# Scheduling the six score products of an attention block as one group over two PSUM banks

## The chip, the cores and the metric

The kernel runs on one core of a Trainium2 chip. The metric is the device time of one execution in microseconds (us), and of several runs the median. The engines are called PE (TensorE, matrix products), DVE (VectorE), ACT (ScalarE), POOL (GpSimd) and SP (which issues the transfers). PE writes its products into PSUM, and a bank of PSUM holds one result of 128 x 512 fp32 numbers. In the lines of the profile, `sc<-qg,qg 64*128 64x512 f16` is a product: into tile `sc`, from two tiles `qg`, 64 rows deep, with 128 columns of weights and 512 moving columns.

## What is computed

The reference is a bidirectional encoder trunk of two layers on 512 tokens of width 1024. Each layer projects the tokens into three groups of heads (differential softmax attention, a gated linear recurrence in both directions, and cross-attention into a memory of 256 tokens), joins them in one output projection and a layer norm, and then runs a gated MLP with a depthwise convolution and a second layer norm. The change concerns the first group:

```python
def diff_attention(q, k, v, lam):          # 4 heads, two components c of width 64 each
    ...
        s = jnp.einsum('bqhcd,bkhcd->bhcqk', qi, k).astype(jnp.float32)
        p = jax.nn.softmax(s, axis=-1)
        a = p[:, :, 0] - lam * p[:, :, 1]
        return jnp.einsum('bhqk,bkhv->bqhv', a.astype(v.dtype), v)
    ...
def hybrid_layer(x, mem, cos, sin, layer, ...):
    proj = x @ w_in
    ...
    mix = jnp.concatenate([da_o, hg_o, mx_o], axis=-1) @ w_out
    x = layer_norm(DEEPNORM_ALPHA * x + mix, ln1_g, ln1_b)
    ...
```

Each head has two score matrices, one per component of width 64, and the second softmax is taken from the first with a weight.

## The kernel before

**Products in three parts.** A number is split into a high and a low fp16 half, and each large product is made of three fp16 products that add up in one PSUM bank: high by high, high by low and low by high (`mm3`, L269, through `mm`, L132; so all of them carry L137 in the profile). Weights arrive as fp32 in tiles `wst` and are scaled and split by ACT and DVE into `wh` and `wl` (`prep`, L250 to L267).

**The score blocks.** `da_attn` (L963) handles two heads of a layer: 2 heads x 4 blocks of 128 queries, so eight blocks, and with two layers and two head pairs there are four such stretches. `scores(i)` (L967) takes two PSUM tiles of tag "sc", one for each component, and writes six products into them: three parts (L978), and for each part the two components (L979 to L981). Component 0 reads rows 0 to 63 of the tiles `qg` and component 1 rows 64 to 127, so one uses the upper and one the lower half of the rows of the array. In program order the two row halves alternate. Then DVE takes the negative maximum of each component (L983) and scales both (L984), and ACT takes the exponentials with their sums (L986), which reads the banks for the last time. `finish` (L989) subtracts the second softmax (L995, DVE), turns the result by four transposes on PE (L996, through L473), and ACT copies it (L997); `values` (L999) multiplies with the values after four blocks.

**What lies beside them.** While a stretch runs, PE also has the projections of the next heads (`gemm_f` and `gemm_t`, tiles `mm<-wh,xh` or `mm<-xh,wh`) and the output products (`down_part`, L514: six products into a tile "mm" for two slices of 128 rows, after which DVE adds the tile to the residual stream, L529; tiles `mm<-wh,mgh`). There are two banks of tag "mm", three of "sc" and two of "tr" (L122).

**What sets the order.** The program is traced once, and a planner then decides the order of the instructions on each engine and which bank each tile gets (`make_plan`, L1520). `extract` (L1232) turns each instruction into an `Op` with a cost in us, the instructions that it depends on, and the list `tiles` of the tiles that it reads or writes. A product with 64 fp16 rows is given a cost of 0.005 us if it follows one on the other row half in program order, and the ordinary cost of 0.216 us otherwise (L1267 to L1275); this is settled before the order is. `deadlines` (L1484) gives PE's instructions due times: the sum of PE's costs in program order; other engines' due times follow from these. `simulate` (L1341) then walks through time. Banks of a tag are handed to tiles in program order (`assign`, L1383). An instruction is offered to its engine once all tiles in its list have a bank and all that it depends on is done (`ntile` and `npred`); of the instructions offered, an engine takes the one that is due first (L1435). A tile's bank goes back when all instructions that list it are done (L1470 to L1477). The order is then fixed by links from each instruction to the next on its engine, and the engines work through it in that order on the chip, each waiting for the data and banks that it needs.

Of the kernel before, what the change touches and what calls it, by code (L numbers as in the profile page):

```python
# [1158 lines left out]
def _esize(dt):  # L1159
    s = str(dt)  # L1160
    return 4 if "32" in s else 2 if "16" in s else 1


def _n(ap):
    n = 1
    for _, c in list(ap)[1:]:
        n *= c
    return n


class Op:
    __slots__ = ("i", "name", "eng", "cost", "tail", "reads", "writes", "table", "preds", "succs", "tiles", "dmab", "line", "kind", "small", "order_ins", "mv", "istr")


def cost_of(i, kind, eng, outs, ins):
# [56 lines left out]
def extract(instrs):  # L1232
    ops = []
    last_half = None
    for i in instrs:
        kind = type(i).__name__
        if kind.startswith("BassTile"):
            continue
        o = Op()
        o.i = len(ops)  # L1240
        o.name = i.name
        o.eng = ENG[str(i.engine).split(".")[-1]]
        o.kind = kind
        o.line = i.debug.lineno if i.debug else 0
        get = lambda xs: [a.bass_ap for a in xs if "AccessPattern" in type(a).__name__]
        outs, ins = get(i.outs), get(i.ins)
        o.order_ins = ins
        o.mv = ins[0] if ins else None
        o.istr = bool(getattr(i, 'is_transpose', False))
        o.table = 0  # L1250
        if kind == "InstActivation":
            o.table = SETS.get(str(i.func).split(".")[-1], 0)
        o.dmab = 0
        if o.eng == "SP":
            b = outs[0]
            n = _esize(b.dtype)
            for _, c in list(b.ap):
                n *= c
            o.dmab = n
            o.cost, o.tail = 0.06, 0  # L1260
        else:
            o.cost, o.tail = cost_of(i, kind, o.eng, outs, ins)
        o.reads = [b for b in ins if type(b.tensor).__name__ == "Tile"]
        o.writes = [b for b in outs if type(b.tensor).__name__ == "Tile"]
        o.preds, o.succs = set(), []
        o.small = _n(outs[0].ap) <= 16 if outs else False
        if o.eng == "PE" and "float16" in str(ins[0].dtype) and ins[0].ap[0][1] == 64:  # L1267
            half = ins[0].offset // ins[0].ap[0][0]
            if last_half not in (None, half):
                o.cost = 0.005  # L1270
                last_half = None
            else:
                last_half = half
        elif o.eng == "PE":
            last_half = None  # L1275
        ops.append(o)

    cache = {}

    def region(b):  # L1280
        t = b.tensor
        es = _esize(b.dtype)
        ap = tuple(tuple(x) for x in b.ap)
        key = (b.offset, ap, es, t.name if False else 0)
        r = cache.get(key)
        if r is None:
            stride = ap[0][0]
            p0, f0 = divmod(b.offset, stride) if stride else (0, b.offset)
            pos = {f0}
            for s, c in ap[1:]:  # L1290
                if s == 0:
                    continue
                pos = {x + s * q for x in pos for q in range(c)}
            m = 0
            if len(pos) == max(pos) - min(pos) + 1:
                lo, n = min(pos) * es, len(pos) * es
                m = ((1 << n) - 1) << lo
            else:
                w = (1 << es) - 1
                for x in pos:  # L1300
                    m |= w << (x * es)
            r = cache[key] = (p0, p0 + ap[0][1], m)
        return r

    hist = defaultdict(list)
    tiles = {}
    for o in ops:
        o.tiles = []
        for wr, bs in ((False, o.reads), (True, o.writes)):
            for b in bs:  # L1310
                t = b.tensor
                nm = t.name
                if nm not in tiles:
                    tiles[nm] = t
                if nm not in o.tiles:
                    o.tiles.append(nm)
                psum = "PSUM" in str(t.space)
                p0, p1, m = region(b)
                h = hist[nm]
                for (j, w2, a0, a1, m2) in h:  # L1320
                    if (wr or w2) and j != o.i:
                        if psum or (a0 < p1 and p0 < a1 and m & m2):
                            o.preds.add(j)
        for wr, bs in ((False, o.reads), (True, o.writes)):
            for b in bs:
                p0, p1, m = region(b)
                h = hist[b.tensor.name]
                psum = "PSUM" in str(b.tensor.space)
                if wr:
                    if psum:  # L1330
                        h[:] = []
                    else:
                        h[:] = [e for e in h if not (p0 <= e[2] and e[3] <= p1 and (e[4] & ~m) == 0 and e[0] != o.i)]
                h.append((o.i, wr, p0, p1, m))
    for o in ops:
        for p in o.preds:
            ops[p].succs.append(o.i)
    return ops, tiles


# [179 lines left out]
def make_plan(instrs):  # L1520
    ops, tiles = extract(instrs)
    _, _, _, order, slot_of = simulate(ops, tiles, deadlines(ops, tiles))
    return list(order.values()), {tiles[t].source_name: s for t, s in slot_of.items()}
# [45 lines left out]
```

## Time and profile before

| what | us |
|---|---|
| median of 3 runs | 1530.95 |
| lowest and highest of them | 1530.77, 1532.63 |
| the profiled execution | 1531.64 |
| its span, from the first to the last instruction | 1529.9 |

The profile is of one execution. A timeline line has the start, the length, the engine, the line of the code, the operation, the tiles, the shape and a count of like instructions merged into one; in square brackets stand the idle time of the engine before it and the instruction whose end it waited for. A line that groups instructions ends with the time in which at least one of them ran, the mean length of one in ns, and the idle time just before them. Products are pipelined, so that one starts before the one ahead of it has ended: the distance of two starts is what a product costs PE, not its length. A line of the view by windows has the window, its length, the busy time and number of instructions of each engine in it, the granted TensorE clock, the share of time in which the transfer engines were busy, and what they moved.

### The profile page before, as it was taken

The page shows a single profiled execution, that of the slowest core. Times are in us where ns is not written, and L with a number is a line of the kernel's source. Part 1 is how long each engine was busy: PE and PEld are TensorE (multiplying, and loading weights), DVE is VectorE, ACT ScalarE, POOL GpSimd, SP SyncE. Part 2 cuts the span into 40 slices and gives each one's busy share as a digit, 9 for nine tenths or more (in the row PEclk, how much of TensorE's full clock was granted, in tenths as well). Part 3 has the DMA queues.
Part 4 walks back from the last instruction along what each step waited for, and adds up shares of the span by engine and source line. Part 5 has one row for each costly group of instructions (what it writes and reads, how often), then busy time and mean ns, then how long its engine had stood idle before and what let it go on. Part 6 is the DMA issues. An engine that isn't in the chain of part 4 may idle for free. (4 is left out here: it accounts for less than half of the span.)

```text
span 1529.9 us, 24770 instructions
## 1 busy us (share of the span) xinstructions
PE 1477.0 (97%) x10072; PEld 824.3 (54%) x10072; DVE 1147.8 (75%) x2133; ACT 862.1 (56%) x1090; POOL 233.7 (15%) x258
## 2 busy tenths in 40 slices
PE   4999999999999999999999999999999999999997
PEld 3766565464574444444478475655555544444443
DVE  7688967778797766775794969668779776676677
ACT  4776566656376555554556555566653756455550
POOL 4131312030011000010110331021201101001001
PEclk9999999999999999999999999999999999999999
DMA  6332221132233233233234312111232433343321
GB/s 217 126 118 84 71 70 56 56 108 75 69 111 110 88 105 110 83 110 103 91 111 139 97 43 84 50 61 56 67 99 62 133 111 91 102 111 94 100 83 55
DMA packets 158141, 141.93 MB, mean 93 GB/s; under 512 B 3286, under 2 KB 139082, under 8 KB 158026
## 3 DMA queue, kind: packets, MB, share of 16 engines
q1 hardware_dynamic: 158026, 140.34, 29.5%
q8 instruction: 79, 1.29, 0.4%
q14 instruction: 36, 0.29, 0.1%
HBM read 138.23 MB, written 2.10 MB: 92 GB/s over the span
## 5 line engine op out<-in xcount | busy, mean ns | idle before, releaser
L137 PEld LDWEIGHTS <-wh 128*128 128x128 f16 x2688 | 256.5, 98 | 232.1 <-issue 2.3
L266 DVE SCALAR_TENSOR_TENSOR wl<-wst,ws,wh 128x2048 f16<-128x2048 f32 x122 | 315.9, 2590 | 73.0 <-ACT wh L265 72.9
L137 PE MATMUL mm<-xh,wl 128*128 128x512 f16 (+1 forms) x832 | 301.7, 363 | 1.3 <-DVE wl L266 1.3
L137 PE MATMUL mm<-xh,wh 128*128 128x512 f16 (+1 forms) x832 | 301.7, 363 | 0.0
L137 PE MATMUL mm<-xl,wh 128*128 128x512 f16 (+1 forms) x832 | 301.4, 363 | 0.0
L262 ACT ACTIVATE wh<-wst 128x2048 bf16<-128x2048 f32 x122 | 232.2, 1903 | 110.2 <-PE stat L165 54.1
L265 ACT ACTIVATE wh<-wst,ws 128x2048 f16<-128x2048 f32 x122 | 243.5, 1996 | 41.6 <-DVE wi L156 25.6
L137 PE MATMUL mm<-wh,t 128*128 128x512 f16 (+1 forms) x768 | 223.1, 370 | 1.7 <-DVE z L529 1.6
L137 PEld LDWEIGHTS <-wl 128*128 128x128 f16 x1344 | 131.4, 98 | 123.3 <-issue 1.9
L137 PEld LDWEIGHTS <-t 128*128 128x128 f16 x1152 | 110.4, 98 | 122.2 <-issue 1.2
L529 DVE SCALAR_TENSOR_TENSOR z<-mm,inv,z 128x512 f32<-128x512 f32 x176 | 130.3, 745 | 47.1 <-PE mm L137 33.3
L137 PE MATMUL sc<-xh,wh 128*128 128x512 f16 (+1 forms) x448 | 156.2, 349 | 1.3 <-ACT xh L247 0.8
L137 PE MATMUL sc<-xl,wh 128*128 128x512 f16 (+1 forms) x448 | 156.2, 349 | 0.0
L137 PE MATMUL sc<-xh,wl 128*128 128x512 f16 (+1 forms) x448 | 156.2, 349 | 0.0
L137 PE MATMUL mm<-wl,t 128*128 128x512 f16 (+1 forms) x384 | 142.1, 370 | 0.0
L1098 POOL TENSOR_TENSOR t<-f 128x512 f32<-128x512 f32 x44 | 58.4, 1328 | 545.3 <-DVE f L1096 429.3
L152 DVE TENSOR_SCALAR we<-stat 128x1 int32<-128x1 int32 x122 | 18.4, 151 | 125.2 <-PE stat L165 125.1
L137 PE MATMUL mm<-wh,mgh 128*128 128x512 f16 x192 | 72.8, 379 | 5.1 <-DVE z L529 2.5
L1094 ACT ACTIVATE f<-sc,cvb,cw 128x512 f32<-128x512 f32 x44 | 34.1, 775 | 71.4 <-PE stat L165 68.8
L137 PE MATMUL mm<-wh,mgl 128*128 128x512 f16 x192 | 72.6, 380 | 0.6 <-DVE gi L156 0.6
L137 PE MATMUL mm<-wl,mgh 128*128 128x512 f16 x192 | 72.8, 379 | 0.0
L137 PE MATMUL mm<-wh,xh 128*128 128x256 f16 x256 | 67.6, 281 | 2.7 <-ACT xh L247 2.7
(224 smaller groups left out, 2188.3 us busy)
## 6 DMA issues: line engine op xcount, KB each, us to landing
wst<-in_w_up_dram SPq DMA_DIRECT2D x88, 512.0 KB, 4.5
wst<-in_w_in_dram SPq DMA_DIRECT2D x36, 1024.0 KB, 5.1
wst<-in_w_down_dram SPq DMA_DIRECT2D x22, 1024.0 KB, 5.0
wst<-in_w_out_dram SPq DMA_DIRECT2D x12, 1024.0 KB, 5.1
wst<-in_w_mem_kv_dram SPq DMA_DIRECT2D x8, 1024.0 KB, 5.7
z<-in_x_dram SPq DMA_DIRECT2D x4, 512.0 KB, 9.6
mix<-in_ln_g_dram SPq DMA_DIRECT2D x4, 512.0 KB
mix<-in_ln_b_dram SPq DMA_DIRECT2D x4, 512.0 KB
```

Source lines behind the costliest of these rows:

```text
L137: T.matmul(o, lhsT, rhs, start=start, stop=stop)
L152: V.tensor_scalar(e, tot.bitcast(I32), 0x7F000000, 1, ALU.bitwise_and, ALU.logical_shift_right)
L262: A.activation(h.rearrange("p a b -> p (a b)").bitcast(BF16), flat, AF.Square, accum_out=ss)
L265: A.activation(h.rearrange("p a b -> p (a b)"), flat, AF.Identity, scale=s)
L266: V.scalar_tensor_tensor(l.rearrange("p a b -> p (a b)"), flat, s, h.rearrange("p a b -> p (a b)"), ALU.mult, ALU.subtract)
L529: V.scalar_tensor_tensor(zs, p_, ivs[half % len(ivs)], zs, ALU.mult, ALU.add)
L1094: A.activation(c, p_, AF.Identity, scale=cw[:, 1, v : v + 1], bias=cvb[:, l, i + 22 * v : i + 22 * v + 1])
L1098: G.tensor_tensor(gt[:, n, :], c2[:, 0, :], c2[:, 1, :], ALU.mult)
```

## The change

The six products of a block get the same list of tiles: both "sc" tiles of the block. So in the planner none of them is offered to PE before both tiles have a bank, and each tile's bank goes back only when all six are done (and its readers). `Op` gets a field for the row half, and the rule for the cost is written in another way with the same result. A new pass at the end of `extract` goes through PE's instructions in program order, gathers runs of products that have a row half, and joins the lists of tiles in groups of six. Instructions, their operands and what they compute stay the same.

```diff
@@ class Op
-    __slots__ = ("i", "name", "eng", "cost", ..., "order_ins", "mv", "istr")
+    __slots__ = ("i", "name", "eng", "cost", ..., "order_ins", "mv", "istr", "half")
@@ def extract
-        if o.eng == "PE" and "float16" in str(ins[0].dtype) and ins[0].ap[0][1] == 64:
-            half = ins[0].offset // ins[0].ap[0][0]
-            if last_half not in (None, half):
-                o.cost = 0.005
+        o.half = None
+        if o.eng == "PE":
+            if "float16" in str(ins[0].dtype) and ins[0].ap[0][1] == 64:
+                o.half = ins[0].offset // ins[0].ap[0][0]
+                if last_half not in (None, o.half):
+                    o.cost, last_half = 0.005, None
+                else:
+                    last_half = o.half
+            else:
                 last_half = None
-            else:
-                last_half = half
-        elif o.eng == "PE":
-            last_half = None
         ops.append(o)
...
     for o in ops:
         for p in o.preds:
             ops[p].succs.append(o.i)
+    run = []
+    for o in ops + [None]:
+        if o is not None and o.eng != "PE":
+            continue
+        if o is not None and o.half is not None:
+            run.append(o)
+            continue
+        for k in range(0, len(run), 6):
+            both = list(dict.fromkeys(t for p in run[k : k + 6] for t in p.tiles))
+            for p in run[k : k + 6]:
+                p.tiles = both
+        run = []
     return ops, tiles
```

More of the change, by code (lines that the diff above doesn't have):

```diff
@@ L1171 @@
 class Op:
-    __slots__ = ("i", "name", "eng", "cost", "tail", "reads", "writes", "table", "preds", "succs", "tiles", "dmab", "line", "kind", "small", "order_ins", "mv", "istr")
+    __slots__ = ("i", "name", "eng", "cost", "tail", "reads", "writes", "table", "preds", "succs", "tiles", "dmab", "line", "kind", "small", "order_ins", "mv", "istr", "half")
 def cost_of(i, kind, eng, outs, ins):
```

## The prediction

> **What bounds the kernel now.** I read the page first, for which engine is full, and then asked the trace for the products that the change names.
>
> ```profile
> span 1529.9 us, 24770 instructions
> PE 1477.0 (97%) x10072; PEld 824.3 (54%) x10072; DVE 1147.8 (75%) x2133; ACT 862.1 (56%) x1090; POOL 233.7 (15%) x258
> ```
>
> TensorE is busy for 1477.0 of 1529.9 us, VectorE for three quarters. Work taken from PE is therefore worth its own length wherever other work is ready to move up; the question is where it is not. The groups by shape give the score products, the only ones with 64 rows:
>
> ```profile
> L137 PE MATMUL sc<-qg,qg 64*128 64x512 f16 x192 | 49.6, 379 | 0.8 <-ACT f L986 0.7
> ```
>
> 192 products are 32 blocks of six (2 layers x 2 head pairs x 8 blocks). They lie in four stretches, each opened by a run of nine. The timeline of PE at the first, and the last of these four runs:
>
> ```profile
> 271.51 1.47 PE L137 MATMUL sc<-qg,qg 64*128 64x512 f16 x9
> 272.91 0.28 PE L137 MATMUL mm<-wh,xh 128*128 128x256 f16 x1
> ...
> 277.93 0.82 PE L137 MATMUL sc<-qg,qg 64*128 64x512 f16 x3
> 278.68 0.28 PE L137 MATMUL mm<-wh,xh 128*128 128x256 f16 x1
> ...
> 1084.31 1.47 PE L137 MATMUL sc<-qg,qg 64*128 64x512 f16 x9
> ```
>
> Nine products hold PE from 271.51 to 272.91, 1.40 us, but three alone hold it for 0.75 (277.93 to 278.68). So the first six of the nine took 0.65 us, 0.22 a pair: they alternated and ran two at a time. The last three are one row half of the second block, because there are three "sc" banks and the first block took two. All later products come in such groups of one half, which cost as much as six would. The groups' busy time confirms the count: four runs at 1.47 and 52 halves at 0.82 make 48.5 us, against 49.6 in the row. The 1.1 us left over are halves cut in two by a transpose, as here:
>
> ```profile
> 290.22 0.39 PE L137 MATMUL mm<-wh,mgh 128*128 128x512 f16 x1
> 290.54 0.60 PE L137 MATMUL sc<-qg,qg 64*128 64x512 f16 x2
> 291.08 0.66 PE L473 MATMUL tr<-cst,f 128*128 128x128 f32 x4
> 291.66 0.39 PE L137 MATMUL sc<-qg,qg 64*128 64x512 f16 x1
> 291.98 0.39 PE L137 MATMUL mm<-wl,mgh 128*128 128x512 f16 x1
> ```
>
> Such a half is busy 0.60 + 0.39 instead of 0.82, 0.17 more, so there are about seven. Only 4 of 32 blocks alternate today.
>
> **The change part by part.** It touches no instruction, only the planner's input: each of a block's six products now lists both PSUM banks, so none is offered to PE before both are free. The costs (0.216 us for the first of a pair, 0.005 for the second) are as before; the plan already charged a block about 0.66 us, and paid for two lone halves on the chip. Due times come from program order and move by one product at most, so I expect the order far from the score blocks to stay much as it is.
>
> *What PE saves.* The price of a lone half, at the end of the first stretch:
>
> ```profile
> 300.99 0.38 PE L137 MATMUL mm<-wh,mgh 128*128 128x512 f16 x1
> 301.21 0.38 PE L137 MATMUL mm<-wl,mgh 128*128 128x512 f16 x1
> ...
> 301.88 0.38 PE L137 MATMUL mm<-xl,wh 128*128 128x512 f16 x1
> 302.19 0.82 PE L137 MATMUL sc<-qg,qg 64*128 64x512 f16 x3
> 302.94 0.39 PE L137 MATMUL mm<-xh,wl 128*128 128x512 f16 x1
> ```
>
> Ordinary products start 0.22 us apart (300.99, 301.21). Before the half there are 0.31, so entering costs 0.09; from its start to the next product there are 0.75. A lone half takes 0.84 us of PE, a block of two 1.69. Six alternating products take 0.65 between their own starts plus about 0.10 on leaving and 0.09 on entering: 0.84 again. A block that now alternates saves 0.84 us. In each stretch six blocks save that. The second block saves 0.65, since its first half now rides behind the run of six without an entry or exit of its own. That is 5.7 us a stretch, 22.8 for four. The seven cuts cost about 0.2 each (one more entry and exit), 1.4; I assume that few new ones arise, since the group is no longer on PE than a half is now. The sum is **24.2 us of PE**.
>
> *What hides it or takes its place.* The other work of the four stretches, from the second block on:
>
> ```profile
> core 0: us, PE busy (x) PEld busy (x) DVE busy (x) ACT busy (x) POOL busy (x), PEclk, DMA share, GB/s
> 278.00:303.00 25.00, 25.00 (x116) 9.41 (x117) 20.12 (x47) 17.45 (x34) 0.00 (x0) 1.00 0.09 30
> 343.00:369.00 26.00, 25.76 (x130) 10.67 (x128) 20.81 (x51) 19.40 (x38) 0.00 (x0) 1.00 0.19 68
> 1024.00:1052.00 28.00, 27.71 (x146) 12.96 (x145) 23.46 (x58) 19.44 (x36) 0.00 (x0) 1.00 0.15 49
> 1088.00:1116.00 28.00, 27.27 (x155) 13.65 (x153) 22.07 (x55) 20.01 (x38) 0.00 (x0) 1.00 0.18 62
> sum 107.00, PE 105.74 PEld 46.70 DVE 86.46 ACT 76.30 POOL 0.00; mean PE 26.43 PEld 11.68 DVE 21.62 ACT 19.08 POOL 0.00
> ```
>
> PE is full here (105.7 of 107), VectorE is the next engine with 86.5. If the same work stays in the stretches they cannot go under 86.5 us: the saving is at most 20.5 of the 24.2, and only with VectorE never idle. How full it gets beside a full PE, two windows show:
>
> ```profile
> 360.00:370.00 10.00, 9.84 (x43) 3.33 (x41) 9.53 (x21) 5.61 (x11) 0.00 (x0) 1.00 0.33 108
> 370.00:380.00 10.00, 8.08 (x53) 5.69 (x53) 9.73 (x24) 5.26 (x9) 0.60 (x2) 1.00 0.53 140
> ```
>
> At 95% of VectorE PE was still full (9.84), at 97% it lost a fifth (8.08). So I take 95%: 86.46 / 0.95 = 91.0 us, a saving of **16 us**. The ends that I keep are 24.2 (fillers that need little VectorE move in, and its work moves out of the stretches) and nothing.
>
> *The wait that is added.* Now the first half of a block starts when one bank is free, and its maximum (L983) is taken while PE does the other half later. With the change both halves wait for the exponential of the block before to free a second bank, and both maxima come after it. The chain in the trace, a half's start to its bank's release:
>
> ```profile
> 282.58 0.69 DVE L983 TENSOR_REDUCE dam<-sc 128x1 f32<-128x512 f32 x1 [0.43 <-PE sc L137]
> ...
> 283.01 0.82 PE L137 MATMUL sc<-qg,qg 64*128 64x512 f16 x3
> ...
> 283.57 0.78 ACT L986 ACTIVATE f<-sc,dam,iqk 128x512 f32<-128x512 f32 x1 [1.08 <-DVE dam L984]
> ...
> 283.87 0.69 DVE L983 TENSOR_REDUCE dam<-sc 128x1 f32<-128x512 f32 x1 [0.33 <-PE sc L137]
> ```
>
> and the group that reads the exponential's sum out, in the view by lines:
>
> ```profile
> L986 ACT ACTIVATION_READ_ACCUMULATOR f<-sc,dam,iqk 128x1 f32 x11 | 2.1, 195 | 0.0
> ```
>
> The products take 0.86 us (283.01 to 283.87), maximum to exponential 0.99 (282.58 to 283.57), the exponential with its sum 0.78 + 0.20: 2.8 us now, and about 3.5 with the second maximum in line. The blocks follow each other at (302.19 - 277.93) / 6 = 4.04 us. The longer chain fits into that pitch with 0.5 us to spare, so I cost it at nothing beside VectorE's limit. Behind the waiting product PE's whole queue stands, but the plan puts other products ahead of the group; what that costs if there is none is the fourth rival.
>
> The sum is made against the profiled execution's 1531.64 us (its span is 1529.9): 1531.64 - 16 = 1515.6. The median of the runs, 1530.95, lies 0.7 below that execution, so I predict **1515 us**.
>
> **The rivals.**
>
> *All of it.* PE finds fillers that need little of VectorE (projections rather than output products), and VectorE's work spreads beyond the stretches: 1530.95 - 24.2 = 1507. For it: VectorE now idles for maxima that PE delivers late:
>
> ```profile
> L983 DVE TENSOR_REDUCE dam<-sc 128x1 f32<-128x512 f32 x12 | 8.3, 691 | 6.6 <-PE sc L137 6.5
> L529 DVE SCALAR_TENSOR_TENSOR z<-mm,inv,z 128x512 f32<-128x512 f32 x7 | 5.2, 746 | 0.1
> ```
>
> (the first stretch). Against it: the fillers are mostly output products, and each six of them (1.30 us of PE) end in a 0.75 us eviction by VectorE. Chance 0.20.
>
> *The banks' readers become the bound.* The longer chain keeps today's waiting in VectorE's and ScalarE's queues, 4.04 - 2.8 = 1.2 us a block, and the pitch grows to about 4.7. PE's freed time must then be filled with output products whose evictions wait in the same VectorE queue. About a third of 24.2 is kept, 8 us: 1523. Against it: VectorE idles for 20.5 of 107 us today. Chance 0.20. The Trainium skill, "TensorEngine Tiling (Array Packing)", section "PSUM Bottleneck", states such a rule: packing the array speeds TensorE up but not the emptying of PSUM, which may then be the limit. No run so far shows it for these blocks.
>
> *It does not do what it says.* If transposes or other products come between the halves in the plan, a block pays two entries again and the pair's overlap is lost; with all blocks cut, nothing changes: 1531. Against it: the six become ready together and PE takes the earliest due, which is the other half each time, as the four opening blocks show. Chance 0.05.
>
> *Slower.* The pitch grows by 0.65 us and PE finds nothing to do in the freed 0.84 + 0.65 = 1.49 us of each block, because the two "mm" banks wait for L529 behind the score work. Where PE idles for more than 0.84 / 1.49 = 56% of that, the block is longer than now. At 75% it costs 28 x (0.75 x 1.49 - 0.84) = 7.8 us: 1539. For it, at the end of the last stretch:
>
> ```profile
> 1120.17 0.38 PE L137 MATMUL mm<-wh,mgh 128*128 128x512 f16 x1 [1.92 <-DVE z L529]
> ```
>
> Against it: this is the longest such wait in the stretches, and after the second one output products remain in stock that need no score of it:
>
> ```profile
> L137 PE MATMUL mm<-wh,mgl 128*128 128x512 f16 x28 | 10.6, 379 | 0.0
> L137 PE MATMUL mm<-wh,mgh 128*128 128x512 f16 x28 | 10.6, 379 | 0.6 <-DVE z L529 0.6
> L137 PE MATMUL mm<-wl,mgh 128*128 128x512 f16 x28 | 10.6, 379 | 0.0
> ```
>
> (370 to 400 us): 84 at 0.22 are 18 us. Chance 0.05.
>
> **How the numbers follow.** The forecast, 1510 to 1520, has 0.50; all of it, to 1506, has 0.20; the readers, 1520 to 1528, have 0.20; no change and slower have 0.05 each. The first three are all faster by more than 0.2% (3 us, about what a measurement of this kernel can tell from no change): 0.90 faster, 0.05 within, 0.05 slower. The range 1506 to 1526 takes in the first two cases and most of the third, and leaves out a little more than one in ten.
>
> **What would show it.** The 64-row products should stand in about 32 runs of six that hold PE for 0.75 us each from first start to the next product, their busy time falling from 49.6 us to some 26 to 28. The four stretches should be 3 to 5 us shorter each, with VectorE at 90% or more. If PE shows new gaps that end with L986 or L529 in them, the readers have taken the gain; if VectorE stays near 80% and PE near 100%, all of it has come. The prediction is wrong if the plan reorders work far from the stretches, or if VectorE cannot keep 95% because its maxima now come in pairs.

## The result and the profile after

| | us, median (lowest to highest) | profiled execution | its span | mean granted clock |
|---|---|---|---|---|
| before | 1531.15 (1530.77 to 1532.63), 4 runs | 1531.64 | 1529.9 | 0.997 |
| after | 1519.86 (1518.66 to 1522.45), 4 runs | 1518.81 | 1517.0 | 0.993 |

After takes 0.9927 of the time of before (95% interval 0.991 to 0.9944): 11.3 us less. That is inside the range of the prediction, and 4.7 us less of a gain than the 16 that it forecast.

The page of after, its span and its busy times:

```profile
span 1517.0 us, 24771 instructions
PE 1458.1 (96%) x10072; PEld 823.6 (54%) x10072; DVE 1148.1 (76%) x2133; ACT 860.2 (57%) x1090; POOL 237.2 (16%) x258
```

PE is busy for 18.9 us less than before (1477.0), and the span is 12.9 shorter. So some 6 us are new time in which PE stands idle. The score products, in the groups by shape:

```profile
L137 PE MATMUL sc<-qg,qg 64*128 64x512 f16 x192 | 28.4, 380 | 0.4 <-ACT f L986 0.3
```

Their busy time fell from 49.6 to 28.4 us. Of the 32 blocks 27 stand in one uncut run of six. The timeline of PE in the first stretch shows how six now cost what three did:

```profile
276.85 0.82 PE L137 MATMUL sc<-qg,qg 64*128 64x512 f16 x6
277.60 0.28 PE L137 MATMUL mm<-wh,xl 128*128 128x256 f16 x1
...
281.30 0.82 PE L137 MATMUL sc<-qg,qg 64*128 64x512 f16 x6
```

From 276.85 to the next product there are 0.75 us, for six products as before for three. The stretches themselves, in the view by windows, one window for each:

```profile
core 0: us, PE busy (x) PEld busy (x) DVE busy (x) ACT busy (x) POOL busy (x), PEclk, DMA share, GB/s
277.00:307.00 30.00, 28.30 (x174) 14.67 (x171) 28.79 (x67) 21.86 (x39) 1.74 (x1) 1.00 0.31 103
340.00:372.00 32.00, 27.20 (x156) 15.80 (x152) 27.57 (x65) 21.69 (x39) 0.00 (x0) 0.89 0.28 88
1018.00:1049.00 31.00, 30.15 (x180) 14.99 (x179) 29.04 (x68) 21.92 (x39) 2.71 (x3) 1.00 0.23 81
1078.00:1110.00 32.00, 28.75 (x181) 15.39 (x177) 29.45 (x66) 22.19 (x41) 1.20 (x2) 1.00 0.31 101
sum 125.00, PE 114.40 PEld 60.85 DVE 114.85 ACT 87.67 POOL 5.65; mean PE 28.60 PEld 15.21 DVE 28.71 ACT 21.92 POOL 1.41
```

VectorE is at 92% (114.85 of 125) and PE at 91.5%, where before PE had 99% and VectorE 81%. What PE waits for, in the view of the waits, before and then after (in all, how often, longest):

```profile
PE mm L137 <- DVE z L529: 4.1, 5, 1.9
```

```profile
PE mm L137 <- DVE z L529: 9.1, 8, 2.7
...
PE tr L243 <- DVE xl L248: 1.9, 1, 1.9
```

**The books.** Gaps between PE's instructions add up to 34.9 us before and 41.6 after. And the granted clock fell to half in two places where before it did not. One window at each, after:

```profile
364.00:371.00 7.00, 6.03 (x30) 5.91 (x30) 4.98 (x13) 2.81 (x6) 0.00 (x0) 0.52 0.82 229
1148.00:1153.00 5.00, 4.23 (x15) 2.08 (x15) 3.83 (x6) 1.37 (x2) 0.00 (x0) 0.66 0.00 0
```

In the records the clock is at half for 6.8 us at the first and 3.4 us at the second. PE is busy in 9.3 of these 10.2 us (the rest is idle time, counted above), and half of that, 4.6 us, is lost. (One further 3.4 us at half speed both kernels have, before at 172 us and after at 77.) So: 23.5 us less PE work, 6.7 more idle, 4.6 more lost to the clock, 0.6 gained ahead of PE's first instruction: 23.5 - 6.7 - 4.6 + 0.6 = 12.8, against 12.9 in the spans. The 23.5 is not measured by itself: it is what the busy time leaves, 18.9 + 4.6. The score products alone show most of it. From each one's start to the next product's start, without idle time, they hold PE for 45.5 us before and 26.1 after, 19.4 less, and the 25 entries that are saved (62 groups before, 37 after), at the 0.09 us of the prediction, add 2.3.

**Where it was lost.** The start of the same product (the k-th of its kind) in both traces, for five places; each figure is the later kernel's time less that of before. Three of the experiments below stand beside it. Each column is one execution, and the four executions of after differ by up to 3.8 us.

| the place, by its time in before | after | e2 | e3 | e9 |
|---|---|---|---|---|
| ahead of stretch 1, 268.14 | -0.7 | -0.6 | -0.7 | 0.0 |
| behind stretch 1, 314.56 | -5.1 | -5.1 | -0.7 | -5.3 |
| behind stretch 2 and the layer norm after it, 474.69 | -5.7 | -2.5 | -6.1 | -10.1 |
| ahead of stretch 4, 1080.93 | -10.2 | -6.7 | -6.2 | -14.7 |
| behind stretch 4 and the layer norm after it, 1208.09 | -12.8 | -6.7 | -8.8 | -22.5 |

Stretches 1 and 3 kept 4.5 us each. Stretch 2 with what follows kept 0.6, stretch 4 with what follows 2.6. Between the same places, stretch 2 with what follows has 2.8 us more idle time of PE than before and loses 2.9 to the clock, and stretch 4 has 0.7 and 1.7; stretch 1 has 1.7 more idle time, stretch 3 has 0.5. The longest single waits inside stretches 2 and 4 are alike, 1.65 and 1.55 us. The one in stretch 2:

```profile
347.91 2.34 DVE L266 SCALAR_TENSOR_TENSOR wl<-wst,ws,wh 128x2048 f16<-128x2048 f32 x1
...
351.75 0.74 DVE L529 SCALAR_TENSOR_TENSOR z<-mm,inv,z 128x512 f32<-128x512 f32 x1
...
352.55 0.38 PE L137 MATMUL mm<-wh,mgh 128*128 128x512 f16 x1 [1.65 <-DVE z L529]
```

The split of a weight tile (L266, 2.34 us) and both maxima of a block stand ahead of the eviction in VectorE's queue. Behind stretches 2 and 4 the output products that are left run beside the first layer norm, and the timeline of after shows what happens there (PE's row is the one that waits):

```profile
405.15 0.73 DVE L529 SCALAR_TENSOR_TENSOR z<-mm,inv,z 128x512 f32<-128x512 f32 x1
...
407.12 1.41 DVE L236 SCALAR_TENSOR_TENSOR z<-z,lnrs,mix 128x512 f32<-128x512 f32 x2
...
410.52 0.38 PE L137 MATMUL mm<-wh,mgl 128*128 128x512 f16 x1
...
411.36 0.75 DVE L236 SCALAR_TENSOR_TENSOR z<-z,lnrs,mix 128x512 f32<-128x512 f32 x1 [0.41 <-POOL lnrs L227]
...
412.09 0.74 DVE L236 SCALAR_TENSOR_TENSOR z<-z,lnrs,mix 128x512 f32<-128x512 f32 x1
...
412.75 0.74 DVE L529 SCALAR_TENSOR_TENSOR z<-mm,inv,z 128x512 f32<-128x512 f32 x1
...
413.55 0.38 PE L137 MATMUL mm<-wh,mgh 128*128 128x512 f16 x1 [2.65 <-DVE z L529]
```

VectorE takes no eviction between 405.15 and 412.75. It works on the layer norm (L235, L236), and even waits for POOL in between (0.41), while both "mm" banks are full and the evictions stand behind in its queue. PE has issued its last product at 410.52 and waits for 2.65 us. In layer 2 PE waits behind stretch 4 as well, but not for an eviction: its transposes (L243) wait for L248, which splits the norm's result on VectorE. Half speed follows at 1149. In e2 (below) the same two waits stand at the norm of layer 1, and there the clock stays full. The lines of after, then those of e2:

```profile
1147.34 0.66 PE L243 MATMUL tr<-cst,z 128*128 128x128 f32 x4 [1.93 <-DVE xl L248]
1148.77 0.27 PE L137 MATMUL sc<-xh,wh 128*128 128x256 f16 x1 [0.78 <-ACT xh L247]
```

```profile
413.73 0.66 PE L243 MATMUL tr<-cst,z 128*128 128x128 f32 x4 [1.93 <-DVE xl L248]
415.16 0.27 PE L137 MATMUL sc<-xh,wh 128*128 128x256 f16 x1 [0.78 <-ACT xh L247]
```

The kernel before waits at the norm of layer 1 as well, for L187, a step of the norm on VectorE:

```profile
420.47 0.38 PE L137 MATMUL mm<-wh,mgh 128*128 128x512 f16 x1 [1.54 <-DVE lnsc L187]
```

So the 2.65 us are idle time that could be won there, and for the greater part not a loss against before.

### The profile page after: what moved, and what is told of

Its sections match the earlier page's. It is cut to its first block, busy times and chain, and to the rows that moved or that the text cites. A ratio compares the mean times of both kernels' runs of the same rounds, so it can differ in the third digit from the quotient of the medians.

```text
span 1517.0 us, 24771 instructions
## 1 busy us (share of the span) xinstructions
PE 1458.1 (96%) x10072; PEld 823.6 (54%) x10072; DVE 1148.1 (76%) x2133; ACT 860.2 (57%) x1090; POOL 237.2 (16%) x258
## 5 line engine op out<-in xcount | busy, mean ns | idle before, releaser
L266 DVE SCALAR_TENSOR_TENSOR wl<-wst,ws,wh 128x2048 f16<-128x2048 f32 x122 | 315.9, 2590 | 72.1 <-ACT wh L265 71.8
L529 DVE SCALAR_TENSOR_TENSOR z<-mm,inv,z 128x512 f32<-128x512 f32 x176 | 129.7, 745 | 46.3 <-PE mm L137 32.8
L986 ACT ACTIVATE f<-sc,dam,iqk 128x512 f32<-128x512 f32 x64 | 49.3, 775 | 37.8 <-DVE dam L984 36.6
```

Source lines behind the costliest of these rows:

```text
L266: V.scalar_tensor_tensor(l.rearrange("p a b -> p (a b)"), flat, s, h.rearrange("p a b -> p (a b)"), ALU.mult, ALU.subtract)
L529: V.scalar_tensor_tensor(zs, p_, ivs[half % len(ivs)], zs, ALU.mult, ALU.add)
L986: A.activation(pe[:, c, :], sc_[c], AF.Exp, bias=mx[:, c : c + 1], scale=iqk, accum_out=z1 if c else z0)
```

## The experiments

Ratios are to the kernel before, with the 95% interval.

**e1: the row halves one after the other.** In the order of after, the six products of a block are placed component by component, within the same places of PE's order.

```diff
+    for k in range(0, len(halves), 6):
+        block = halves[k : k + 6]
+        places = sorted(at[i] for i in block)
+        for p, i in zip(places, sorted(block, key=lambda i: (ops[i].half, i))):
+            pe[p] = i
```

> The changed kernel's order on every engine, but inside the places of a block's six products component 0's three come first and then component 1's three, so that no two run at a time. Theory 'two at a time' (the gain is PE time): a block costs PE 0.65 us more, 32 blocks 20.8 us, of which up to 12 us can go into waits that PE now has in the stretches: 1529 to 1541 us. Rival 'the order' (the gain comes from the other instructions' new order or the banks' new hand-out): it stays at 1520 us.

Measured: 1520.39 us, 0.9925 (0.991 to 0.9939), the same as after. But it does not show what it was made for. The timeline of e1:

```profile
278.65 0.83 PE L137 MATMUL sc<-qg,qg 64*128 64x512 f16 x6
```

The six still take 0.83 us. Their single starts lie 10, 215, 10, 206 and 10 ns apart, and the second to start carries the wait that in e8 stands with component 1's first product. So it is a product of component 1, ahead of two of component 0 that were placed before it. The trace doesn't record the place in PE's queue; that PE changed the order is inferred from this wait, and from e8, where an order set in the same way was kept. So e1 separates nothing, except that the alternation in the plan is not needed when the six stand together.

**e8: the halves apart.** Component 1's three products are put one full-height product behind component 0's.

```diff
+        seq = sorted(block, key=lambda i: (ops[i].half, i))
+        pe[at[0] : end] = seq[:3] + between + seq[3:]
```

> The changed kernel's order on every engine, but component 1's three products of a block stand one full-height product behind component 0's three, so that the halves cannot meet in the array whatever PE does with products that stand next to each other. Theory 'side by side' (a block is cheap when its six products stand together, in either order): a block costs PE 0.84 us more again, 32 blocks 27 us, of which up to 12 us fall into waits and half clock that the changed kernel has: 1535 to 1547 us. Rival 'the order' (the other instructions' new order brought the gain): it stays at 1520 us.

Measured: 1540.81 us, 1.0056 (1.0043 to 1.007): 20.9 us slower than after, and slower than before. The timeline of e8:

```profile
278.32 0.82 PE L137 MATMUL sc<-qg,qg 64*128 64x512 f16 x3
279.07 0.28 PE L137 MATMUL mm<-wh,xl 128*128 128x256 f16 x1
279.28 0.82 PE L137 MATMUL sc<-qg,qg 64*128 64x512 f16 x3
280.03 0.18 PE L165 MATMUL stat<-wss,ones 128*128 128x1 bf16 x1
```

One product in between is enough: each half costs 0.75 again. With the wait for both banks kept and the pairing gone, the gain is gone too. So the pairing brings the gain. The 9.7 us over before are not the price of the group alone: e8 also takes apart the four opening blocks, which before ran in pairs, PE's gaps are 3.3 us longer (38.2), and the clock is at half for 17.1 us where before has 3.4.

**e2 and e3: the group in half of the stretches.** e2 groups the blocks of stretches 1 and 3 alone (first head pair), e3 those of 2 and 4.

```diff
         for k in range(0, len(run), 6):
+            block += 1
+            if (block - 1) // 8 % 2 != 0:
+                continue
```

> Only the blocks of the first head pair of each layer (stretches 1 and 3) are scheduled as groups; those of stretches 2 and 4 are left as they were before. Theory 'the stretch's fillers decide' (projections follow stretches 1 and 3, so nearly all of PE's saving comes through there; stretches 2 and 4 have only output products, whose bank must be emptied by VectorE, and give most of it back): 9 us of the 11 stay, 1521 to 1523 us. Rival 'each stretch gives the same': half, 1525.5 us.

> The other half: only the blocks of stretches 2 and 4 are groups. Theory 'the stretch's fillers decide': 2 to 4 us of gain, 1527 to 1529 us, with the second stretch giving about nothing and TensorE's clock at half for some microseconds after it. Rival 'each stretch gives the same': 1525.5 us.

Measured: e2 1525.88 us, 0.996 (0.9948 to 0.9972); e3 1525.02 us, 0.9955 (0.9943 to 0.9966). The theory that the kind of filler decides, with 1522 and 1528, fell. In the medians the two gains, 5.3 and 6.1, add up to that of after. The table above shows that they do not arise where they should: e2 gains 4.5 us in stretch 1 and has lost 2.6 of them behind stretch 2, which is not changed in it; what it has ahead of stretch 4, 6.7, it keeps. e3 keeps 5.4 us in stretch 2, where after keeps 0.6. Of that difference 2.9 us are the clock: in after it fell in stretch 2, in e3 it did not, though the half speed behind stretch 2 was expected of e3.

**e4: VectorE's load, by moving work.** The subtraction of the second softmax (L995) goes to POOL as two instructions.

```diff
-                    V.scalar_tensor_tensor(pe[:, 0, :], pe[:, 1, :], z1, pe[:, 0, :], ALU.mult, ALU.add)
+                    G.tensor_tensor(pe[:, 1, :], pe[:, 1, :], z1.broadcast_to([P, 512]), ALU.mult)
+                    G.tensor_tensor(pe[:, 0, :], pe[:, 1, :], pe[:, 0, :], ALU.add)
```

> The changed kernel, with the difference of the two softmaxes (L995, 0.74 us of VectorE for each block) done by two operations on GpSimd, which is idle in the stretches. Theory 'VectorE is what PE waits for' (evictions L529 stand behind its other work): VectorE is rid of 32 x 0.66 = 21 us, PE's new waits of some 7 us and the half clock after the second stretch mostly go: 1511 to 1516 us. Rival 'the chain of the banks' (products to maxima to exponentials to the bank): that chain doesn't hold L995, so the time stays at 1520 us, or rises since the transposes come up to 2 us later.

Measured: 1522.98 us, 0.9939 (0.9927 to 0.9951). The gain that a full VectorE predicts did not come. It is not a clean test: 10 blocks instead of 5 are cut, and the score products are busy for 31.6 us instead of 28.4.

**e11 and e13: VectorE's load, by leaving work out.** e11 keeps the order of after and shortens the same instruction from 512 to 8 columns on the chip (the planner sees the full width), so the rest of the second softmax is left out; e13 does that to the kernel before.

```diff
+                    w = 512 if slots is None else 8
-                    V.scalar_tensor_tensor(pe[:, 0, :], pe[:, 1, :], z1, pe[:, 0, :], ALU.mult, ALU.add)
+                    V.scalar_tensor_tensor(pe[:, 0, :w], pe[:, 1, :w], z1, pe[:, 0, :w], ALU.mult, ALU.add)
```

> The changed kernel with its order on every engine unchanged, but L995 works on 8 of 512 columns, so that VectorE is rid of about 0.5 us for each of 32 blocks without any other engine getting work (the rest of the second softmax is left out of the result). Theory 'VectorE is what PE waits for': PE's idle time in the four stretches falls by 5 to 8 us and the half clock with it, 1509 to 1514 us. Rival 'the banks' chain' (products, maxima, exponentials, bank): L995 is not in that chain, 1518 to 1521 us.

> The kernel before, its order unchanged, with L995 on 8 of 512 columns (the rest of the second softmax is left out of the result). Theory 'PE was the bound before': VectorE's lighter load brings 0 to 3 us, 1528 to 1531. Rival 'VectorE bounds the stretches in both kernels': as much as in e11_short.

Measured: e11 1518.09 us, 0.9912 (0.9897 to 0.9928), 1.8 us less than after; e13 1531.14 us, 0.9996 (0.9987 to 1.0005). The windows of e11 at the same times as those of after, and its waits:

```profile
sum 125.00, PE 115.68 PEld 61.78 DVE 108.69 ACT 89.04 POOL 6.80; mean PE 28.92 PEld 15.45 DVE 27.17 ACT 22.26 POOL 1.70
```

```profile
PE mm L137 <- DVE z L529: 8.8, 8, 2.6
```

VectorE has 6.2 us less to do in the stretches (108.69 for 114.85) and is at 87%. PE's waits for evictions stay, 8.8 us for 9.1, and all its gaps go from 41.6 to 39.2. So VectorE's load is not what cost most of the rest of the gain.

**e9, e12, e10: VectorE's order.** In the planner every VectorE instruction that touches an "mm" tile is due 12 us earlier (e9) or 6 (e12), and so goes ahead of other work that is ready. e10 does the same with 12 to the kernel before.

```diff
-    _, _, _, order, slot_of = simulate(ops, tiles, deadlines(ops, tiles))
+    due = deadlines(ops, tiles)
+    for o in ops:
+        if o.eng == "DVE" and any(tiles[t].tag.startswith("mm_") for t in o.tiles):
+            due[o.i] -= 12
+    _, _, _, order, slot_of = simulate(ops, tiles, due)
```

> The changed kernel, but the planner puts VectorE's instructions that empty an 'mm' bank (L529 and others) 12 us earlier in its due times, so that they go ahead of the score work. Theory 'VectorE's order' (PE's new waits come from evictions that stand behind other work in VectorE's queue, not from too much of that work): PE's idle time in stretches 2 and 4 falls by 4 to 7 us and the clock's half-speed stretch behind stretch 2 goes: 1511 to 1516 us. Rival 'VectorE's load' or 'the banks' chain': the score blocks come later instead and the time stays within 2 us of 1520.

> As e9_evict, with evictions 6 us earlier in the due times instead of 12. Theory 'VectorE's order': between the changed kernel and e9_evict, 1508 to 1515 us. Rival 'a lucky plan' (any other order may come out faster or slower by some microseconds): anything from 1507 to 1522, with no order between 0, 6 and 12.

> The same new due times in the kernel before the change, without groups. Theory 'the waits were hidden': there PE is late with lone halves and the evictions are done in time anyway, so the time stays within 3 us of 1531. Rival 'the due times help by themselves': it falls as much as from the changed kernel, to 1523 to 1527.

Measured: e9 1507.84 us, 0.9845 (0.9832 to 0.9859), 12.0 less than after, the fastest of all and 3 us below what was expected. e12 1512.88 us, 0.9879 (0.9866 to 0.9893), between the two. e10 1523.96 us, 0.9951 (0.9939 to 0.9964). The timeline of e9 at the layer norm behind stretch 2:

```profile
405.89 0.75 DVE L236 SCALAR_TENSOR_TENSOR z<-z,lnrs,mix 128x512 f32<-128x512 f32 x1
...
406.55 0.75 DVE L529 SCALAR_TENSOR_TENSOR z<-mm,inv,z 128x512 f32<-128x512 f32 x1
...
407.21 0.74 DVE L236 SCALAR_TENSOR_TENSOR z<-z,lnrs,mix 128x512 f32<-128x512 f32 x1
```

An eviction now stands between the two L236, and the wait of 2.65 us is gone. Between the products that start at 408.46 and at 434.40 in after, e9's lead grows from 1.2 to 3.2 us; across the layer norm behind stretch 4 it grows from 4.5 to 9.7. There the wait of 1.93 us and the half speed that followed it are both gone. In the whole trace of e9 PE's gaps are 35.0 us for 41.6, and its time at half speed is 6.8 us for 13.6: 6.6 us of idle time less and 3.2 us less lost to the clock, together 9.8, where the spans differ by 9.6 (1517.0 and 1507.4). Half of the 3.2 is the fall at 77 us, far ahead of the stretches. The fall in stretch 2, which was expected to go, is still there (6.8 us, at 363). Not every wait for an eviction went. The view of e9's waits:

```profile
PE mm L137 <- DVE z L529: 7.2, 10, 1.5
```

There are ten, where after has eight, but each is short; those of 1.5 us inside stretches 2 and 4 are in both kernels, so an earlier due time did not move these two.

e10 shows that the order was costing the kernel before, too: the time there falls by 7.2 us, which was the rival's forecast. So 7.2 of e9's 12.0 us have nothing to do with the group, and 4.8 do. With evictions early on both sides the group is worth 1523.96 - 1507.84 = 16.1 us, for 11.3 without.

## Why the prediction came out as it did

**What PE saves: right, to some 2 us.** 24.2 us were worked out from the lone half's 0.84; 23.5 is what the books leave, and the score products alone show 21.7 (19.4 + 2.3). The busy time of the score products, forecast at 26 to 28, is 28.4. Few new cuts were assumed, and five blocks are cut, which cost some 2.5 us. e8 confirms that it is the pairing and not another move of the plan.

**What hides it: wrong in cause and in place, and sized too small.** This is the step that failed. I capped the gain by VectorE's load in the four stretches, at 95% of 91 us, and so gave back 24.2 - 16 = 8. What was given back is 11.3 (6.7 + 4.6), and VectorE is in fact at 92% in the stretches. But a VectorE with 6.2 us less to do there brings 1.8 us (e11), and another order of the same work on VectorE brings 12.0 us (e9), of which 4.8 belong to the group. So the order, and not the load, is shown for these 4.8 us. For the rest of the 11.3 the runs name only the places. Most of the 11.3 lies in the second and the fourth stretch and what follows them (0.6 and 2.6 us kept, for 4.5 in each of the others). There the trace shows evictions that stand behind L266 in VectorE's queue, at waits that neither e9 nor e11 removed, and falls of the clock. Seen from PE, an engine that is full and one that does the wrong thing first look alike: both rows say "PE mm <- DVE z L529".

That the time fell inside the range is in part luck: the cap that set the forecast is not what held the kernel, and 1519.86 lies nearer to the 1523 of "the banks' readers" than to my 1515.

**The clock: not foreseen at all.** 4.6 of the 11.3 us are lost at half speed, in places where before ran at full clock. At the first one, after's timeline of PE reads:

```profile
361.35 0.16 PE L165 MATMUL tr<-gss,ones 128*128 128x1 bf16 x1 [1.26 <-ACT mgh L496]
361.83 0.29 PE L430 MATMUL tr<-cst,crow 88*128 88x88 f32 x1 [0.32 <-ACT t L997]
362.06 1.33 PE L137 MATMUL sc<-qg,qg 64*128 64x512 f16 x6
363.85 0.27 PE L430 MATMUL tr<-cst,crow 44*128 44x44 f32 x1 [0.45 <-DVE daz L993]
365.09 6.51 PE L137 MATMUL tr<-tokv,t 128*128 128x128 f32 x32 [0.97 <-DVE cvw L431]
```

There are 2.0 us of idle time in three pieces within 4 us, then the clock falls (at 363.89), and after a fourth piece the 32 transposes take 6.51 us; in stretch 4 of the same trace, at full clock, they take 3.84 (at 1101.22). The wait for ACT's L496 was there before as well (0.84 us, at 373.37, with 0.52 behind it) and cost no clock there.

The idle time alone does not decide it. The waits of 1.93 and 0.78 us go with a fall in after and with none in e2, in the lines above. Ahead of the 32 transposes of stretch 2, e3 has three pieces of idle time (0.94, 0.28 and 0.85 us) and full clock; e9 has almost the same three (0.90, 0.28 and 0.85) and 6.8 us at half speed. Nor is it the group alone: at this place e13, in the order of before, fell for 3.4 us and e10, without groups, for 6.8, while e3 and e4, with stretch 2 grouped, did not fall there. Over all runs the mean granted clock is still lower after, 0.991 to 0.993, than before, 0.994 to 0.999.

**The wait that is added: wrong in what it does, right in that it costs little.** I had the longer chain fit a pitch of 4.04 us and the stretches 3 to 5 us shorter. The pitch grew: from 276.85 in the fence above to the last block's first product at 306.07 six blocks take 29.2 us, 4.87 each, and the four stretches are 35.7, 37.3, 36.5 and 35.9 us long from first to last score product, where they were 31.1, 28.7, 33.2 and 30.9. So the pitch of 4.7 of the rival "the banks' readers" came true, and its time of 1523 missed by 3 us, where mine missed by 5; its new gaps that end with L529 came too. PE found other products for most of the longer pitch, and in e9 the first stretch is 42.8 us long in the fastest kernel of all. The Trainium skill, "TensorEngine Tiling (Array Packing)", section "PSUM Bottleneck", which was cited for that rival, warns that emptying PSUM may become the limit once the array is packed. The trace agrees as far as PE's waits for L529 go, 4.1 us before and 9.1 after. e9 and e11 add that the place of these evictions in the reader's queue could be mended, and that a lighter load did little.

**The other rivals.** "All of it" (1507) needed output products whose evictions cost nothing; it is almost e9's time, 1507.84, but e9 gets there with 7.2 us that have nothing to do with the group. "Does not do what it says" and "slower" did not come; PE did find work for the longer pitch.

**What stays open.** The books tell how much is idle time and how much is clock, but no run holds one of them fixed, so the two can't be priced apart. Why the clock fell at 364 after and not at 374 before isn't settled. No run moves the evictions ahead of L266 in stretches 2 and 4, so what these waits of 1.65 and 1.55 us cost in the end is not shown either. And e4 can't tell whether POOL's version would gain with the blocks uncut.

## What to carry to other kernels

Two products on different row halves overlapped here when all of a group stood next to each other in PE's queue, in either order (six in 0.75 us); one full-height product between the halves lost the whole of it (0.75 us for each three), so look for it in the distance of starts, not in the busy time alone. When a full engine is relieved, look for the instructions that empty its banks and for what stands ahead of them in their own queue, everywhere until the freed work has drained, and test order and load apart: here 6 us less load brought 1.8 us, and an earlier place brought 12.0, and 7.2 to the kernel before. Run such an edit on the kernel before as well, or its whole gain is put down to the change. Look at the granted clock behind each gap in PE: two gaps of 2.7 us in all stood ahead of a loss of 1.7 in after, and the same two cost nothing in e2.

## What was not expected of the hardware

**PE changed the order of products.** In e1 a product of the other row half started ahead of two that stood before it, 10 ns behind the first, as far as the recorded waits tell. The Trainium skill, "TensorE: Matmul & The Clock Gate", Part 3, holds that products keep their order and only weight loads are pulled ahead; e1's starts (10, 215, 10, 206, 10 ns) and its time, 1520.39 for 1519.86, speak against that for products on different row halves.

**The clock fell behind scattered idle time.** Three gaps of 0.32 to 1.26 us, with products between them, stood ahead of 6.8 us at half speed, and one of 1.93 with one of 0.78 behind it ahead of 3.4; in e2 the second pair left the clock full. The same page, Part 1, has half speed follow an idle window of about 3.4 us. The lengths at half speed agree with that figure (3.4 and twice 3.4); the idle time ahead of them, in pieces that are all shorter, does not. Its section "A second HAM failure mode: psum-queue depth-cycling" tells of short idle times between groups of products that lower the clock, and that is nearer to what these rows show.
